# RWKV block inverses through DRAM: scratch laid out by row, block, column, each matrix read back with one transfer

## The chip, the core and the metric

The kernel runs on one core of a Trainium2 chip. The metric is the device time of one execution in microseconds (us). TensorE is called PE here (PEld is its weight load), VectorE DVE, ScalarE ACT, GpSimd POOL, and SP is the engine whose queue issues most DMAs.

## The reference

Two layers of a decoder trunk are computed in float32 on 512 tokens of width 1024. Each layer has a SwiGLU half-step, a mixer (four FoX attention heads, eight RWKV-7 heads, four MoBA heads), a cross attention and a second half-step. The change lies in RWKV-7, whose recurrence is:

```python
def step(state, inp):
    r_t, w_t, k_t, v_t, kk_t, a_t = inp
    sa = jnp.einsum('bhij,bhj->bhi', state, -kk_t)
    state = (state * w_t[:, :, None, :] + sa[..., None] * (kk_t * a_t)[:, :, None, :]
             + v_t[..., None] * k_t[:, :, None, :])
    return state, jnp.einsum('bhij,bhj->bhi', state, r_t)
...
_, ys = lax.scan(step, state0, xs)
```

## The kernel before

**Chunks.** The recurrence is worked in 8 chunks of 64 tokens, for two heads at a time. A pair of heads is called `hp` (0 to 3), so with two layers there are eight episodes, called e0 to e3 (first layer) and e4 to e7 (second layer) below. In each, 16 unit-triangular matrices of 64x64 (8 chunks by 2 heads) have to be inverted.

**Through DRAM.** `rwkv_gram` makes these matrices in the tile `G` (DVE, L721). They are written to a DRAM scratch `scA` (L726, two transfers). From there the four 16x16 blocks on each diagonal are read into `A16` (L730, four transfers), so that the 64 partitions of `A16` hold 4 places by 16 matrices. POOL inverts all of these by back substitution, 30 instructions at L282, and makes a transposed copy (L742). Eight transfers (L746) put the 16x16 inverses on the diagonals of two other scratches that hold zeros elsewhere: `scT` for the transposes, `scP` for the inverses. Then the whole 64x64 matrices come back as `Tf` and `Pf`, tiles of 128 partitions (two heads of 64 rows) by 8 chunks by 64 columns. Each is read at L749 with two transfers of 64 partitions, 128 KB each. All of these transfers are issued by SP, in order, and so are the weight loads (L130), 512 KB each into a ring of three buffers `wraw`.

**After it.** `rwkv_inverse` goes from 16x16 to 64x64 with small matmuls: L809 reads `Tf`, L818 and L826 read `Pf`. PE works strictly in the order of its instructions, so what stands behind L809 waits when L809 waits. Projections (L152 to L154, L948 to L950) fill PE between these steps. Every weight block is split by ACT (`whi`, L145) and DVE (`wlo`, L146) before use.

**The order.** The sequence of the parts is the string `ORDER` and a table of priorities. From these a scheduler sets the order of the instructions on each engine, with its own estimate of how long each takes. So an edit of a transfer can move instructions on engines that it does not touch.

Of the kernel before, what the change touches and what calls it, by code (L numbers as in the profile page):

```python
# [6 lines left out]
F32 = mybir.dt.float32  # L7
# [8 lines left out]
P = 128  # L16
# [75 lines left out]
H = (slice(0, 64), slice(64, 128))  # L92
# [23 lines left out]
class Trunk:  # L116
# [304 lines left out]
    def make_scratch(self, tmp):  # L421

        z = tmp.tile([P, S], F32, name="zs", tag="zs")
        self.nc.gpsimd.memset(z, 0.0)
        self.scA = [self.tc.dram_tile([2, 8, 64, 64], F32, name=f"scA{i}") for i in range(2)]
        self.scP = [self.tc.dram_tile([2, 8, 64, 64], F32, name=f"scP{i}") for i in range(2)]
        self.scT = [self.tc.dram_tile([2, 8, 64, 64], F32, name=f"scT{i}") for i in range(2)]
        for sc in self.scP + self.scT:
            self.nc.gpsimd.dma_start(sc.rearrange("h c s t -> (h c s t)").rearrange("(p n) -> p n", p=P), z)

    def derive_params(self, const):
        nc = self.nc
# [269 lines left out]
    def rwkv_gram(self, l, hp, st):  # L702

        nc, rw = self.nc, self.rw
        ps = lambda c=8: self.bank(TAGS["g"], c)
        mm = nc.tensor.matmul
        ER, B = st["ER"], st["B"]

        G = st["G"] = rw.tile([P, 16, 64], F32, name="G", tag="G")

        BN = st["BN"] = rw.tile([P, 8, 4, 64], F32, name="BN", tag="BN")
        for q in range(2):
            pg = [ps(4).rearrange("p c (i t) -> p c i t", i=2) for h in range(2)]
            for c in range(4):
                g, i = 2 * q + c // 2, c % 2
                for h in range(2):
                    mm(pg[h][:, c].rearrange("p i t -> p (i t)"), B[H[h], g, 2 * i:2 * i + 2].rearrange("p a b -> p (a b)"),  # L717
                       ER[H[h], g, 1:3] if i == 0 else ER[H[h], g, 0:4:3], start=True, stop=True)
            for h in range(2):
                for i, dst in ((0, G[:, 8 * h + 4 * q:8 * h + 4 * q + 4]), (1, BN[:, 4 * q:4 * q + 4, 1 + h])):  # L720
                    nc.vector.tensor_tensor(dst, pg[h][:, :, i], self.gmask[:, i:i + 1, :].to_broadcast([P, 4, 64]), op=ALU.mult)  # L721
            yield

        scA, scP, scT = (x[hp % 2] for x in (self.scA, self.scP, self.scT))
        for a in range(2):
            nc.sync.dma_start(scA[a].rearrange("j s t -> s j t"), G[H[a], 1 - a::2])  # L726
        A = rw.tile([64, 16, 16], F32, name="A16", tag="A16")
        for q in range(4):
            d = slice(16 * q, 16 * q + 16)
            nc.sync.dma_start(A[d], scA.rearrange("a j s t -> (a j) s t")[:, d, d])  # L730
        I = rw.tile([64, 16, 16], F32, name="P16", tag="P16")
        tmp = rw.tile([64, 16, 16], F32, name="T16", tag="T16")
        If = I.rearrange("p a b -> p (a b)")
        nc.gpsimd.memset(If, 0.0)
        nc.gpsimd.memset(If[:, 0:256:17], 1.0)
        for u in range(15, 0, -1):
            n = 16 - u
            self.tt("sub", tmp[:, 0:u, 0:n], A[:, 0:u, u:u + 1].to_broadcast([64, u, n]),
                    I[:, u:u + 1, u:16].to_broadcast([64, u, n]), ALU.mult)
            self.tt("sub", I[:, 0:u, u:16], I[:, 0:u, u:16], tmp[:, 0:u, 0:n], ALU.subtract)  # L740
        It = rw.tile([64, 16, 16], F32, name="I16", tag="T16")
        nc.gpsimd.tensor_copy(It, I.rearrange("p a b -> p b a"))  # L742
        for name, sc, src in (("Tf", scT, It), ("Pf", scP, I)):
            for q in range(4):
                d = slice(16 * q, 16 * q + 16)
                nc.sync.dma_start(sc.rearrange("a j s t -> (a j) s t")[:, d, d], src[d])  # L746
            st[name] = rw.tile([P, 8, 64], F32, name=name, tag=name)
            for a in range(2):
                nc.sync.dma_start(st[name][H[a]], sc[a].rearrange("j s t -> s j t"))  # L749
        yield  # L750

    def rwkv_rows(self, l, hp, st):
# [604 lines left out]
```

## Time and profile before

| | |
|---|---|
| median of 3 runs | 2575.36 us (2575.05 to 2586.14) |
| the profiled execution's own time | 2590.88 us |
| its span | 2589.1 us |
| mean granted TensorE clock | 0.974 |
| busy share of the span | PE 96%, PEld 78%, DVE 52%, ACT 33%, POOL 19% |
| DMA packets | 434880, 218.41 MB |

A busy share says how long an engine had an instruction in work. The granted clock is the share of TensorE's full speed that the chip allowed. Its two levels are 1.2 and 2.4 GHz, which the rows show as 0.50 and 1.00. A wait is put down to the instruction or transfer that ended last before the waiting instruction began.

### The profile page before, as it was taken

The numbers are of one execution on the slowest core, as the hardware profiler recorded it, in microseconds if no ns is written. First come the engines' busy times: TensorE is split into PE (matmuls) and PEld (weight loads), VectorE is DVE, ScalarE is ACT, GpSimd is POOL, SyncE is SP. The second block draws the span as 40 slices with busy tenths as digits, with TensorE's granted clock in tenths as the row PEclk, the third lists the DMA queues.
The fourth block names the chain that finished last, engine by engine and source line by source line (L and its number), as shares of the span: only waits on it lengthen the run. The fifth ranks groups of instructions, "written<-read, shape, count | busy, mean of one in ns | idle before, by whom it ended". The sixth has DMA issues, their size and how long they took to land.

```text
span 2589.1 us, 35163 instructions
## 1 busy us (share of the span) xinstructions
PE 2497.2 (96%) x13976; PEld 2025.7 (78%) x13976; DVE 1346.6 (52%) x2503; ACT 846.9 (33%) x1337; POOL 493.0 (19%) x610
## 2 busy tenths in 40 slices
PE   8999998899999899999999999999999899999999
PEld 7888876787667788888888888767877677888887
DVE  6444445666755654344444444465666666543444
ACT  4222233233343342222332222333333433422222
POOL 4212120232210122020221211202322110221211
PEclk9999999998889999999999999999978999999999
DMA  4333342221213133333333333422212121333332
GB/s 143 104 98 94 96 130 69 66 59 43 64 34 92 53 96 90 104 93 98 95 94 100 94 98 94 121 75 58 67 34 56 56 78 45 110 98 98 95 95 88
DMA packets 434880, 218.41 MB, mean 84 GB/s; under 512 B 63856, under 2 KB 428828, under 8 KB 434716
## 3 DMA queue, kind: packets, MB, share of 16 engines
q1 hardware_dynamic: 431948, 212.36, 28.9%
q10 hardware_dynamic: 2448, 2.76, 0.3%
q8 instruction: 110, 1.80, 0.3%
q0 software_dynamic: 320, 1.05, 0.1%
q14 instruction: 54, 0.44, 0.1%
HBM read 205.64 MB, written 10.49 MB: 83 GB/s over the span
## 4 chain that ended last, share of the span: by engine, by line
PE 86%; DVE 6%; POOL 3%; DMA 2%; ACT 2%; issue 1%; SPq 1%; POOLq 0%; ACTq 0%; DVEq 0%
PE acc L152 22%; PE acc L154 22%; PE acc L153 22%; PE po L1046 2%; PE sp L1034 1%; POOL P L282 1%; PE pt L1022 1%; PE acc L950 1%; PE acc L948 1%; PE acc L949 1%; POOL T L282 1%; DVE wlo L146 1%; ACT whi L145 1%; PE ts L857 1%; PE ty L717 1%
## 5 line engine op out<-in xcount | busy, mean ns | idle before, releaser
L145 ACT ACTIVATE whi<-wraw 128x1024 fp32r<-128x1024 f32 (+3 forms) x386 | 390.3, 1013 | 1142.0 <-PE acc L153 1043.3
L152 PE MATMUL acc<-xh,whi 128*128 128x512 f32 (+1 forms) x1776 | 699.9, 394 | 21.9 <-DVE p L496 7.3
L154 PE MATMUL acc<-xh,wlo 128*128 128x512 f32 (+1 forms) x1776 | 695.8, 392 | 1.3 <-DVE wlo L146 1.3
L153 PE MATMUL acc<-xl,whi 128*128 128x512 f32 (+1 forms) x1776 | 694.8, 391 | 0.0
L146 DVE TENSOR_TENSOR wlo<-wraw,whi 128x1024 fp32r<-128x1024 f32 (+3 forms) x386 | 540.3, 1401 | 100.3 <-ACT whi L145 91.4
L152 PEld LDWEIGHTS acc<-xh,whi 128*128 128x128 f32 (+1 forms) x1776 | 334.4, 188 | 97.6 <-ACT whi L145 9.1
L154 PEld LDWEIGHTS acc<-xh,wlo 128*128 128x128 f32 (+1 forms) x1776 | 334.2, 188 | 75.5 <-DVE wlo L146 2.6
L153 PEld LDWEIGHTS acc<-xl,whi 128*128 128x128 f32 (+1 forms) x1776 | 334.6, 188 | 69.7
L342 POOL TENSOR_TENSOR up<-up,g 128x512 f32<-128x512 f32 x88 | 118.4, 1346 | 999.2 <-ACT whi L145 901.1
L152 PE MATMUL acc<-th,whi 128*128 128x512 f32 x704 | 274.4, 391 | 1.0 <-ACT whi L145 1.0
L154 PE MATMUL acc<-th,wlo 128*128 128x512 f32 x704 | 275.0, 392 | 0.2
L153 PE MATMUL acc<-tl,whi 128*128 128x512 f32 x704 | 274.0, 389 | 0.0
L295 DVE SCALAR_TENSOR_TENSOR x<-acc,x 128x512 f32<-128x512 f32 x96 | 66.0, 691 | 277.2 <-PE acc L154 277.2
L341 DVE TENSOR_TENSOR up<-acc,rsb 128x512 f32<-128x512 f32 x88 | 60.8, 691 | 278.5 <-PE acc L154 278.5
L338 DVE TENSOR_TENSOR g<-acc,rsb 128x512 f32<-128x512 f32 x88 | 60.8, 691 | 191.0 <-PE acc L154 188.0
L154 PEld LDWEIGHTS acc<-th,wlo 128*128 128x128 f32 x704 | 132.1, 188 | 31.5 <-DVE wlo L146 4.2
L152 PEld LDWEIGHTS acc<-th,whi 128*128 128x128 f32 x704 | 132.2, 188 | 30.5 <-ACT whi L145 4.0
L153 PEld LDWEIGHTS acc<-tl,whi 128*128 128x128 f32 x704 | 132.2, 188 | 27.4
L240 POOL TENSOR_TENSOR sqacc<-sqacc,sq 128x512 f32<-128x512 f32 x48 | 75.4, 1571 | 381.6 <-ACT sq L239 245.9
L346 POOL TENSOR_TENSOR tl<-up,th 128x512 fp32r<-128x512 f32 x88 | 128.5, 1461 | 65.5 <-ACT th L345 65.5
L345 ACT ACTIVATE th<-up 128x512 fp32r<-128x512 f32 x88 | 55.8, 634 | 120.8 <-POOL up L342 120.8
L948 PE MATMUL acc<-whi,xh 128*128 128x256 f32 x256 | 76.9, 300 | 0.7 <-DVE zt L520 0.7
(351 smaller groups left out, 3109.1 us busy)
## 6 DMA issues: line engine op xcount, KB each, us to landing
wraw<-in_ffn_w_in_dram SPq DMA_DIRECT2D x176, 512.0 KB
wraw<-in_ffn_w_out_dram SPq DMA_DIRECT2D x64, 512.0 KB
wraw<-in_mix_w_in_dram SPq DMA_DIRECT2D x52, 512.0 KB
wraw<-in_ffn_w_out_dram SPq DMA_DIRECT2D x32, 384.0 KB
wraw<-in_xattn_w_kv_dram SPq DMA_DIRECT2D x16, 512.0 KB
wraw<-in_mix_w_out_dram SPq DMA_DIRECT2D x16, 384.0 KB
scx<-x SPq DMA_DIRECT2D x16, 256.0 KB
x<-scx SPq DMA_DIRECT2D x16, 256.0 KB
```

What stands on the lines that cost most here:

```text
L145: nc.scalar.activation(hv, v, AF.Copy)
L146: nc.vector.tensor_sub(lv, v, f32(hv))
L152: mm(ps, lh, rh, start=start, stop=False)
L153: mm(ps, lh, rl, start=False, stop=False)
L154: mm(ps, ll, rh, start=False, stop=stop)
L240: (nc.vector if m == KC - 1 else nc.gpsimd).tensor_tensor(self.sqacc, self.sqacc, sq, op=ALU.add)
L295: self.nc.vector.scalar_tensor_tensor(xm, ps, coef, xm, op0=ALU.mult, op1=ALU.add)
L338: nc.vector.tensor_tensor(g, pss[0], rsb, op=ALU.mult)
L341: nc.vector.tensor_tensor(up, pss[1], rsb, op=ALU.mult)
L342: nc.gpsimd.tensor_tensor(up, up, g, op=ALU.mult)
L346: nc.gpsimd.tensor_tensor(tl, up, f32(th), op=ALU.subtract)
L948: mm(o, a, wh[:, kk, :], start=k == 0, stop=False)
```

## The change

All scratches get the layout row, block, column: `[64, 16, 64]` instead of `[2, 8, 64, 64]`. The writes and the reads of the 16x16 blocks address the same bytes in the new places, with as many transfers and the same 64-byte runs. The writes of `scA` stay two. Each of `Tf` and `Pf` is read with one transfer of 128 partitions by 2 KB instead of two transfers of 64 partitions by 8 runs of 256 bytes. The source of that transfer is addressed as head, row, run: outermost 2, then 64, then 512 contiguous floats. The destination is 128 partitions by 512 floats.

```diff
-        self.scA = [self.tc.dram_tile([2, 8, 64, 64], F32, name=f"scA{i}") for i in range(2)]
-        self.scP = [self.tc.dram_tile([2, 8, 64, 64], F32, name=f"scP{i}") for i in range(2)]
-        self.scT = [self.tc.dram_tile([2, 8, 64, 64], F32, name=f"scT{i}") for i in range(2)]
+        self.scA = [self.tc.dram_tile([64, 16, 64], F32, name=f"scA{i}") for i in range(2)]
+        self.scP = [self.tc.dram_tile([64, 16, 64], F32, name=f"scP{i}") for i in range(2)]
+        self.scT = [self.tc.dram_tile([64, 16, 64], F32, name=f"scT{i}") for i in range(2)]
...
         for a in range(2):
-            nc.sync.dma_start(scA[a].rearrange("j s t -> s j t"), G[H[a], 1 - a::2])
+            nc.sync.dma_start(scA[:, 8 * a:8 * a + 8], G[H[a], 1 - a::2])
...
-            nc.sync.dma_start(A[d], scA.rearrange("a j s t -> (a j) s t")[:, d, d])
+            nc.sync.dma_start(A[d], scA[d, :, d].rearrange("s j t -> j s t"))
...
-                nc.sync.dma_start(sc.rearrange("a j s t -> (a j) s t")[:, d, d], src[d])
+                nc.sync.dma_start(sc[d, :, d].rearrange("s j t -> j s t"), src[d])
             st[name] = rw.tile([P, 8, 64], F32, name=name, tag=name)
-            for a in range(2):
-                nc.sync.dma_start(st[name][H[a]], sc[a].rearrange("j s t -> s j t"))
+            nc.sync.dma_start(st[name].rearrange("p j t -> p (j t)"), sc.rearrange("s (a j) t -> a s (j t)", a=2))
```

In the changed file every line behind L748 has a number lower by one, so that L808 is the old L809 and L817 the old L818.

SP's queue in e0, from the writes of the inverses to the weight load behind the reads, before:

```order
L746 DMA scP_376<-P_3333 16x16x16 x3
L746 DMA scT_378<-I_3367 16x16x16 x4
L746 DMA scP_376<-P_3333 16x16x16
L749 DMA Tf<-scT_378 64x8x64 x2
L749 DMA Pf<-scP_376 64x8x64 x2
L130 DMA wraw<-in_mix_w_in_dram 128x4x256
```

And the same place in the changed kernel:

```order
L746 DMA scP_376<-P_3333 16x16x16 x3
L746 DMA scT_378<-I_3367 16x16x16 x4
L746 DMA scP_376<-P_3333 16x16x16
L748 DMA Tf<-scT_378 128x1x512
L748 DMA Pf<-scP_376 128x1x512
L130 DMA wraw<-in_mix_w_in_dram 128x4x256
```

The four reads have become two, and nothing else moved here.

PE in e1, from the first matmul that reads `Tf` on (`tk` is the operand made of `G`, `gs` and `g` belong to the output gate of e0), before:

```order
L809 MATMUL ty<-Tf,tk_4123 64x64
L948 MATMUL acc<-whi,xh 128x256
L949 MATMUL acc<-whi,xl 128x256
L950 MATMUL acc<-wlo,xh 128x256
L809 MATMUL ty<-Tf,tk_4123 64x64 x15
L924 MATMUL ts<-ident,tk_4379 128x128 x4
L930 MATMUL ts<-gs_2923,g_4335 128x512
L931 MATMUL ts<-gs_2962,g_4335 128x512
L672 MATMUL tx<-ident,e 128x128 x4
L948 MATMUL acc<-whi,xh 128x256
```

And the same place in the changed kernel:

```order
L808 MATMUL ty<-Tf,tk_4119 64x64 x16
L947 MATMUL acc<-whi,xh 128x256
L948 MATMUL acc<-whi,xl 128x256
L949 MATMUL acc<-wlo,xh 128x256
L923 MATMUL ts<-ident,tk_4375 128x128 x4
L929 MATMUL ts<-gs_2923,g_4331 128x512
L930 MATMUL ts<-gs_2962,g_4331 128x512
L672 MATMUL tx<-ident,e 128x128 x4
L817 MATMUL ty<-tk_4139,Pf 32x16 x16
L825 MATMUL ty<-Pf,tk_4139 64x32 x16
```

All matmuls that read `Tf` now stand together at the front, and those that read `Pf` follow at once. Before, eleven projection matmuls of 128x256 stood between L672 and L818.

SP's queue in e3, before (the first row is two weight loads, of the cross attention's keys and values):

```order
L130 DMA wraw<-in_xattn_w_kv_dram 128x8x128 x2
L746 DMA scP_377<-P_5536 16x16x16 x3
L746 DMA scT_379<-I_5570 16x16x16 x4
L746 DMA scP_377<-P_5536 16x16x16
L749 DMA Tf<-scT_379 64x8x64 x2
L749 DMA Pf<-scP_377 64x8x64 x2
```

And the same place in the changed kernel:

```order
L130 DMA wraw<-in_xattn_w_kv_dram 128x8x128
L746 DMA scP_377<-P_5530 16x16x16 x3
L746 DMA scT_379<-I_5564 16x16x16 x4
L746 DMA scP_377<-P_5530 16x16x16
L130 DMA wraw<-in_xattn_w_kv_dram 128x8x128
L748 DMA Tf<-scT_379 128x1x512
L748 DMA Pf<-scP_377 128x1x512
```

One weight load of 512 KB has moved from ahead of the writes to just ahead of the reads.

## Rows read from the trace of the kernel before

**Rows 1.** The page: the shares of the span that the chain of work that ended last spent, by engine.

```profile
PE 86%; DVE 6%; POOL 3%; DMA 2%; ACT 2%; issue 1%; SPq 1%; POOLq 0%; ACTq 0%; DVEq 0%
```

**Rows 2.** The waits of PE over the whole span: waiting line, what released it, us in total, how often, the longest.

```profile
PE ty L809 <- DMA Tf<-scT: 9.4, 6, 3.9
```

**Rows 3.** The chain of work that ended last, in order of time, around the read of `Tf` in e0: start, us, what (a DMA counts from its issue to the work that it releases).

```profile
494.36 3.00 DMA Tf<-scT
...
497.40 0.69 PE ty L809 x7
```

**Rows 4.** The timeline of SP's queue: the issues of `Tf`'s two transfers in each of the eight episodes e0 to e7 (start, us until both are issued).

```profile
493.71 1.28 SPq L749 DMA_DIRECT2D Tf<-scT  x2
...
568.49 1.28 SPq L749 DMA_DIRECT2D Tf<-scT  x2
...
628.75 1.29 SPq L749 DMA_DIRECT2D Tf<-scT  x2
...
702.49 1.27 SPq L749 DMA_DIRECT2D Tf<-scT  x2
...
1774.60 1.28 SPq L749 DMA_DIRECT2D Tf<-scT  x2
...
1848.93 1.28 SPq L749 DMA_DIRECT2D Tf<-scT  x2
...
1907.49 1.28 SPq L749 DMA_DIRECT2D Tf<-scT  x2
...
1980.63 1.28 SPq L749 DMA_DIRECT2D Tf<-scT  x2
```

**Rows 5.** The timeline of PE: where the matmuls that read `Tf` (L809) and the first that read `Pf` (L818) begin, with PE's idle time before them in brackets, in e0 to e7.

```profile
496.64 0.33 PE L809 MATMUL ty<-Tf,tk 64*64 64x64 f32 x2 [2.52 <-DMA Tf<-scT]
497.40 0.91 PE L809 MATMUL ty<-Tf,tk 64*64 64x64 f32 x12 [0.43 <-DMA Tf<-scT]
506.64 0.68 PE L818 MATMUL ty<-tk,Pf 32*32 32x16 f32 x32
...
571.42 0.29 PE L809 MATMUL ty<-Tf,tk 64*64 64x64 f32 x2 [1.11 <-DMA Tf<-scT]
577.66 0.68 PE L818 MATMUL ty<-tk,Pf 32*32 32x16 f32 x32
...
637.98 0.32 PE L809 MATMUL ty<-Tf,tk 64*64 64x64 f32 x2
643.38 0.68 PE L818 MATMUL ty<-tk,Pf 32*32 32x16 f32 x32
...
708.70 1.97 PE L809 MATMUL ty<-Tf,tk 64*64 64x64 f32 x32
711.65 0.86 PE L818 MATMUL ty<-tk,Pf 32*32 32x16 f32 x32
...
1778.28 1.01 PE L809 MATMUL ty<-Tf,tk 64*64 64x64 f32 x14 [0.41 <-DMA Tf<-scT]
...
1851.83 0.30 PE L809 MATMUL ty<-Tf,tk 64*64 64x64 f32 x2 [1.04 <-DMA Tf<-scT]
...
1920.44 0.33 PE L809 MATMUL ty<-Tf,tk 64*64 64x64 f32 x2
...
1986.21 1.15 PE L809 MATMUL ty<-Tf,tk 64*64 64x64 f32 x32
```

**Rows 6.** The DMA view: the queue of the transfers that ACT issues (packets, MB, share of 16 engines), and all transfers issued on it (count, KB each).

```profile
q10 hardware_dynamic: 2448, 2.76, 0.3%
...
mtk<-in_mem_dram ACTq DMA_DIRECT2D x2, 1024.0 KB
...
lw<-in_rwkv_w_dram ACTq DMA_DIRECT2D x8, 32.0 KB
lw<-in_rwkv_a_dram ACTq DMA_DIRECT2D x8, 32.0 KB
...
gm<-in_moba_q_gain_dram ACTq DMA_DIRECT2D x2, 32.0 KB
gm<-in_moba_k_gain_dram ACTq DMA_DIRECT2D x2, 32.0 KB
...
fb<-in_fox_f_bias_dram ACTq DMA_DIRECT2D x2, 0.0 KB
...
pstage<-in_ffn_norm_dram ACTq DMA_DIRECT2D x1, 8.0 KB
```

**Rows 7.** Stretches with DMA traffic: us, busy time of each engine (instructions), granted clock, mean busy share of the 16 DMA engines, GB/s. First eight loads of `x` (128 partitions by 2 KB each), then one store of the same shape, then the reads of `Tf` and `Pf` in e0 (256-byte runs).

```profile
758.00:763.00 5.00, 5.00 (x33) 3.99 (x31) 1.67 (x6) 2.85 (x10) 2.99 (x3) 0.81 0.96 329
...
374.12:374.92 0.80, 0.80 (x5) 0.64 (x5) 0.71 (x2) 0.41 (x1) 0.31 (x1) 1.00 0.84 325
...
495.00:498.00 3.00, 0.93 (x14) 0.79 (x16) 2.69 (x13) 0.00 (x0) 0.10 (x1) 0.85 0.82 181
```

**Rows 8.** The same view for the stretch behind PE's wait in e0 and for the one behind its wait in e1 (granted clock is the third number from the end).

```profile
497.00:504.00 7.00, 6.60 (x41) 5.52 (x42) 1.22 (x6) 0.60 (x1) 0.00 (x0) 0.51 0.62 174
...
574.00:580.00 6.00, 6.00 (x88) 4.32 (x87) 4.82 (x8) 0.74 (x1) 1.38 (x1) 1.00 0.18 54
```

**Rows 9.** From the timeline of ACT in e0, the split of a weight block, and from the chain of work in order of time, one projection matmul of 128x256 (start, us, what).

```profile
516.84 1.06 ACT L145 ACTIVATE whi<-wraw 128x1024 fp32r<-128x1024 f32 x1 [0.97 <-PE acc L153]
...
518.74 0.12 PE acc L948
```

More of the change, by code (lines that the diff above doesn't have):

```diff
@@ L424, in make_scratch @@
         self.nc.gpsimd.memset(z, 0.0)
-        self.scA = [self.tc.dram_tile([2, 8, 64, 64], F32, name=f"scA{i}") for i in range(2)]
-        self.scP = [self.tc.dram_tile([2, 8, 64, 64], F32, name=f"scP{i}") for i in range(2)]
-        self.scT = [self.tc.dram_tile([2, 8, 64, 64], F32, name=f"scT{i}") for i in range(2)]
+        self.scA = [self.tc.dram_tile([64, 16, 64], F32, name=f"scA{i}") for i in range(2)]
+        self.scP = [self.tc.dram_tile([64, 16, 64], F32, name=f"scP{i}") for i in range(2)]
+        self.scT = [self.tc.dram_tile([64, 16, 64], F32, name=f"scT{i}") for i in range(2)]
         for sc in self.scP + self.scT:
-            self.nc.gpsimd.dma_start(sc.rearrange("h c s t -> (h c s t)").rearrange("(p n) -> p n", p=P), z)
+            self.nc.gpsimd.dma_start(sc.rearrange("s j t -> (s j t)").rearrange("(p n) -> p n", p=P), z)
     def derive_params(self, const):
```

## The prediction

> **What bounds the kernel now.** First the page: PE is 86% of the chain that ended last, DMA 2% [rows 1]. So a transfer counts only where PE stands still for it. The waits of PE show how often that is: L809 waits for `Tf` in 9.4 us altogether [rows 2]. The chain around e0 shows how the wait is made up: the second of the two transfers is issued at 494.36, lands 3.00 us later, and L809 goes on at 497.40 [rows 3]. The timelines of SP and PE then give the slack of each episode. In e0, e1, e4 and e5 PE is there before `Tf` (idle 2.52 and 0.43 in e0, 1.11 in e1, similar in the second layer). In e2, e3, e6 and e7 L809 starts without a wait, 9.2, 6.2, 13.0 and 5.6 us behind the first issue [rows 4, 5]. L818, which needs `Pf`, waits nowhere.
>
> **What is removed.** Per episode two issues of some 0.64 us on SP (1.28 for a pair [rows 4]), and, for each matrix, 896 of 1024 packets (128 runs of 2 KB in place of 1024 of 256 bytes). If nothing else changed, `Tf` would be whole one issue earlier: the start of the chain moves from 494.36 to 493.71 in e0. That is the gain that the first rival below has in full.
>
> **What the new read costs.** The question is over how many DMA engines it is spread. The ACT queue shows how that is decided. Its transfers have 2 x 256 runs of `mtk`, 16 x 64 rows of `lw`, 4 x 128 rows of `gm`, 16 rows of `pstage` and 2 x 4 floats of `fb`: 2072 pieces. The queue counts 2448 packets [rows 6]. The 376 left over are 23 x 16 + 2 x 4. I read them as one completion mark for each engine used: sixteen for every transfer of 16 rows or more, but four for `fb`, whose outermost count is 4. With sixteen for each the queue would count 2472. So a transfer is dealt out by the outermost dimension, and one with a short outermost dimension runs on few engines. The new read has 2 outermost in its source and 128 in its destination. Two source entries can be dealt to two engines, so I take two. No row shows a transfer with unequal counts; that is what is uncertain.
>
> The Trainium skill states the rule for just that case (DMA: Bandwidth & Descriptors, section on why a DMA increments its semaphore by 16 and not by 1): the number of engines is the largest one up to 16 that divides the outermost count of both sides, which gives two here. The count of `fb` agrees; the unequal case is shown by no run so far. By that rule the sum below stands as it is; by the other rule of that page it would be the first rival's.
>
> On two engines each carries 128 KB of `Tf`, then 128 KB of `Pf`, since SP issues them one after the other into the same queue. The rate of one engine with 2 KB runs: 329 GB/s over 16 x 0.96 is 21.4 GB/s for loads, 325 over 16 x 0.84 is 24.2 for stores [rows 7]. I take the middle, 22.8, because two engines press on the memory less than sixteen at 96%: 131072 B are 5.75 us. The fixed part of a read is 3.00 less the data part now: 8 KB per engine at 181/(16 x 0.82) = 13.8 GB/s [rows 7], 0.6 us, so 2.4. **`Tf` is there 8.2 us behind the first issue, `Pf` 13.9 us**, instead of about 3.7 for `Tf`.
>
> PE's added idle time for `Tf`, ready time against the start that the rows give [rows 4, 5]:
> - e0: 493.71 + 8.2 = 501.9 against 497.40: 4.5. e4: 1774.60 + 8.2 against 1778.28: 4.5.
> - e1: 576.7 against 571.42: 5.3. The three matmuls that lay between the halves of `Tf` before now stand behind it, so all of it is idle. e5: 1857.1 against 1851.83: 5.3.
> - e2: 636.95 against 637.98, where the new order asks some 1.6 us earlier (thirteen projection matmuls of 128x256, at 0.12 us each [rows 9], no longer stand ahead of it): 0.6. e6: 1915.7 against 1920.44: 0.
> - e3: 710.7 against 708.70, asked 0.7 us earlier in the new order (six such matmuls): 2.7. Here a weight load now stands ahead of the reads on SP. It is 32 KB per engine, at 21.4 GB/s 1.5 us if the read lies wholly behind it, 0 if it is over; I take 0.8. e7: 1988.8 against 1986.21, 2.6.
>
> Together 26.3 us. `Pf` comes into play where L818 follows soon after L809. In e0 it is ready at 507.6, and L818 would stand at 506.64 + 4.5: no wait. In e1 it is ready at 582.4 and wanted at 577.66 + 5.3 - 1.3 (the eleven matmuls that moved behind it [rows 9]) = 581.7: 0.7. In e3 it is ready at 717.2 and wanted at 711.65 + 3.5: 2.0. The second layer is taken as the first: 5.4 us in all.
>
> **The clock.** Behind PE's wait in e0 the granted clock is 0.51 over 7 us (the level of 1.2 GHz), so 3.4 us of work are lost there; behind the wait of 1.11 in e1 it stays at 1.00 [rows 8]. With 5.3 us of idle time I expect e1 and e5 to lose the same, and e7 too; e3 ran on a low clock already, which the 1.97 us of its L809 against 1.15 in e7 shows [rows 5]. Three stretches are 10.2 us. While PE is slow it comes to L818 later, so the 3.4 us of waits for `Pf` in e1, e5 and e7 are within this: 6.8 more. If no stretch is added, it is nothing.
>
> **At nothing.** Weight loads issued behind the reads share the two queues and land up to 11 us later; the first one behind e0's reads (issued at about 496.4) is the next but one to be split, at 516.84 [rows 9], 20 us on, so I count none of it. If that cover were gone, it would cost up to those 11 us an episode. The writes of the blocks keep their count and run length; their new addresses could cost nothing, or at most double a data part of 0.6 us in each of three steps, 1.8 us in each of the four episodes that PE waits for. I take nothing. The moves of instructions are work that PE does in either order.
>
> **Sum.** 26.3 + 5.4 + 6.8 = 38.5 us. The profiled execution took 2590.88 us, 15.5 above the median of the runs; the difference is made within the one execution, and I add it to the median: 2575.4 + 38.5 = **2614 us**, 1.5% slower.
>
> **The rivals.**
> - *Spread over sixteen engines* (dealt by the 128 partitions of the destination). Each engine has 16 KB, 0.75 us, so `Tf` is ready 3.2 us behind the first issue: 496.9 instead of 497.4 in e0. In e0, e1, e4 and e5 PE gains 0.5 us each: 2573 us, no change that can be told. For it: each of the 128 rows goes to a partition of its own, and all large transfers of before run on sixteen. Against it: the marks of `fb`. The Trainium skill has a rule that would give this time (DMA: Bandwidth & Descriptors, Rules for kernel authors): two transfers to disjoint halves of the partitions gain nothing over one of 128. In this kernel it would hold if the one transfer kept its sixteen engines.
> - *Sixteen engines and the clock held.* The same 0.5 us earlier, and the idle time of e0 and e4 gets short enough that their two low stretches of 3.4 us do not come: 2575.4 - 2 - 6.8 = 2567, on the other side of before. It decides if PE's wait in e0 falls from 2.95 us to something like the 1.11 of e1, at which the clock stayed. Half a microsecond does not do that.
> - *Two engines, but hidden.* PE would have to have other work ahead of L809. The order gives it less: in e1, e2 and e3 L809 and L818 stand earlier. Only e2 and e6 hide it. With the fast rate of 24.2 and no clock stretch the sum is still about 27 us: 2602.
>
> **How the numbers follow.** 0.5% (12.9 us) is about what a measurement of this kernel can tell from no change. Two engines: 0.79, nearly all of it slower; its own range is 2598 (fast rate, no clock) to 2630 (21.4 GB/s, a stretch more, late weight loads). Sixteen engines: 0.17, no change. Faster: 0.04. The range that leaves out no more than 2 in 10 reaches down to the second case: 2572 to 2632. Slower 0.78, same 0.18, faster 0.04.
>
> **What would show it.** In the profile after, L808 waits for `Tf` some 35 us instead of 9.4, in all but e2 and e6, and the DMA view shows a low busy share with long duration during the reads (2 of 16 engines, 0.13 plus other traffic). From the issue of `Tf` to L808 in e0 it is 8 us; 3.2 would make the step on the two engines wrong, and with it the forecast. The packets, 434880 before, fall by 16 x 896 = 14336 for the reads; with them go 32 x 16 = 512 completion marks, and 16 x 2 = 32 come if the reads run on two engines, 256 if on sixteen: 14816 fewer in all, or 14592. The granted clock behind e1 and e5 is at 0.50 for some 7 us; if it stays at 1.00, that term is wrong. If other waits of PE shrink as L808's grows, the sum is too large.

## The result and the profile after

| | before | changed |
|---|---|---|
| median | 2580.75 us (4 runs, 2575.05 to 2596.5) | 2620.35 us (4 runs, 2606.84 to 2626.09) |
| profiled execution: own time, span | 2590.88, 2589.1 us | 2626.09, 2624.4 us |
| mean granted clock | 0.974 | 0.968 |

The ratio of the runs is 1.0142, with a 95% interval of 1.0112 to 1.0172: the change makes the kernel 1.4% slower. (The two medians of the table alone differ by 39.6 us, 1.5%.)

The page of the changed kernel, the count of packets and the chain that ended last by engine (against [rows 1]):

```profile
DMA packets 420065, 218.42 MB, mean 83 GB/s; under 512 B 46992, under 2 KB 411964, under 8 KB 419900
...
PE 86%; DVE 4%; DMA 4%; POOL 2%; ACT 2%; issue 1%; SPq 1%; ACTq 0%; POOLq 0%; DVEq 0%
```

DMA has doubled its share of the chain, from 2% to 4%. The packets fell by 434880 - 420065 = 14815.

The waits of PE in the changed kernel (waiting line, what released it, us in total, how often, the longest); the first line answers to [rows 2]:

```profile
PE ty L808 <- DMA Tf<-scT: 34.8, 6, 8.7
...
PE ty L817 <- DMA Pf<-scP: 5.2, 2, 3.1
```

The wait for `Tf` went from 9.4 to 34.8 us, and a wait for `Pf` is new. The chain in order of time around the read of `Tf` in e0 (answers to [rows 3]):

```profile
498.57 8.12 DMA Tf<-scT
...
506.73 1.33 PE ty L808 x19
```

The timeline of PE, with the idle time before an instruction in brackets: the first matmuls that read `Tf` (L808) and, where they waited, those that read `Pf` (L817), in e0 to e5 and e7 (answers to [rows 5]):

```profile
506.73 1.97 PE L808 MATMUL ty<-Tf,tk 64*64 64x64 f32 x32 [7.91 <-DMA Tf<-scT]
...
585.83 1.97 PE L808 MATMUL ty<-Tf,tk 64*64 64x64 f32 x32 [6.73 <-DMA Tf<-scT]
...
647.76 1.15 PE L808 MATMUL ty<-Tf,tk 64*64 64x64 f32 x32
...
716.30 1.97 PE L808 MATMUL ty<-Tf,tk 64*64 64x64 f32 x32 [3.16 <-DMA Tf<-scT]
721.49 0.68 PE L817 MATMUL ty<-tk,Pf 32*32 32x16 f32 x32 [2.17 <-DMA Pf<-scP]
...
1806.97 1.97 PE L808 MATMUL ty<-Tf,tk 64*64 64x64 f32 x32 [8.71 <-DMA Tf<-scT]
...
1885.65 1.98 PE L808 MATMUL ty<-Tf,tk 64*64 64x64 f32 x32 [6.53 <-DMA Tf<-scT]
...
2015.45 1.15 PE L808 MATMUL ty<-Tf,tk 64*64 64x64 f32 x32 [1.80 <-DMA Tf<-scT]
2020.64 1.04 PE L817 MATMUL ty<-tk,Pf 32*32 32x16 f32 x32 [3.06 <-DMA Pf<-scP]
```

PE waits for `Tf` in every episode but e2 (its row has no bracket) and e6. The duration behind the start shows the clock: 1.97 us for the 32 matmuls at the lower level, 1.15 at the upper.

Where the time went is read from stretches: us, busy time of PE, PEld, DVE, ACT and POOL (instructions), granted clock, DMA share, GB/s. First before, from the first write of `scA` in a layer to that layer's cross attention, for layer 1 and layer 2:

```profile
467.80:889.20 421.40, 396.31 (x3147) 313.50 (x3147) 259.21 (x674) 150.36 (x302) 84.74 (x166) 0.93 0.22 60
...
1747.20:2172.10 424.90, 398.69 (x3147) 319.44 (x3147) 258.01 (x675) 150.33 (x302) 83.19 (x165) 0.92 0.22 60
```

The same stretches of the changed kernel, and then the times around and behind PE's waits in e0 and e1:

```profile
472.50:913.80 441.30, 402.30 (x3147) 320.36 (x3147) 258.10 (x674) 149.96 (x302) 85.81 (x166) 0.90 0.21 57
...
1771.90:2207.30 435.40, 396.63 (x3146) 315.80 (x3146) 258.26 (x675) 149.64 (x302) 83.92 (x165) 0.92 0.21 58
...
499.00:507.00 8.00, 0.27 (x5) 0.27 (x6) 3.79 (x14) 0.58 (x1) 0.45 (x3) 0.63 0.37 105
...
501.00:511.00 10.00, 4.27 (x38) 3.67 (x39) 1.79 (x10) 0.60 (x1) 0.10 (x1) 0.51 0.47 138
...
583.00:589.00 6.00, 3.17 (x38) 3.08 (x39) 0.00 (x0) 0.81 (x2) 0.00 (x0) 0.50 0.35 111
```

The two stretches grew by 441.3 - 421.4 = 19.9 and 435.4 - 424.9 = 10.5 us, 30.4 of the 35.3 by which the span grew. Length less PE's busy time is its idle time: 25.1 to 39.0 and 26.2 to 38.8, together 26.5 us more. The other 3.9 us are busy time (6.0 more in layer 1, 2.1 less in layer 2), the same instructions at a lower or higher clock. The last 4.7 us of the span lie ahead of the first write of `scA`, where both kernels have the same transfers and instructions in the same order; they are no effect of the change, and show how far two executions differ by themselves. During the read of e0 PE worked 0.27 of 8 us, and the DMA engines had a share of only 0.37.

### The profile page after: what moved, and what is told of

Its sections match the earlier page's. It is cut to its first block, busy times and chain, and to the rows that moved or that the text cites. A ratio compares the mean times of both kernels' runs of the same rounds, so it can differ in the third digit from the quotient of the medians.

```text
span 2624.4 us, 35148 instructions
## 1 busy us (share of the span) xinstructions
PE 2507.0 (96%) x13976; PEld 2033.6 (77%) x13976; DVE 1347.9 (51%) x2503; ACT 845.7 (32%) x1337; POOL 493.1 (19%) x610
## 2 busy tenths in 40 slices
DMA packets 420065, 218.42 MB, mean 83 GB/s; under 512 B 46992, under 2 KB 411964, under 8 KB 419900
## 4 chain that ended last, share of the span: by engine, by line
PE 86%; DVE 4%; DMA 4%; POOL 2%; ACT 2%; issue 1%; SPq 1%; ACTq 0%; POOLq 0%; DVEq 0%
PE acc L152 22%; PE acc L154 22%; PE acc L153 22%; PE po L1045 2%; DMA Tf<-scT 1%; PE sp L1033 1%; PE acc L947 1%; PE acc L948 1%; PE pt L1021 1%; PE acc L949 1%; ACT whi L145 1%; DMA Pf<-scP 1%; PE ts L856 1%; POOL P L282 1%; DVE wlo L146 1%
```

## The experiments

**One transfer of 128 rows on sixteen engines.** The changed kernel has a new order, one transfer for two, and (by the forecast) two engines for sixteen. This run keeps the first two (the order nearly; in SP's queue a weight load now stands between the two reads of e0) and addresses the source as 128 runs in the order of their addresses, so that the rows land in other partitions.

```diff
-            nc.sync.dma_start(st[name].rearrange("p j t -> p (j t)"), sc.rearrange("s (a j) t -> a s (j t)", a=2))
+            nc.sync.dma_start(st[name].rearrange("p j t -> p (j t)"), sc.rearrange("s j t -> (s j t)").rearrange("(p n) -> p n", p=P))
```

> The changed kernel, but each of Tf and Pf is read as 128 contiguous pieces of 2 KB, one per partition: still one transfer, same size, same run length, same place in SP's queue and nearly the same order on PE; only the source's outermost count is 128 instead of 2. The rows land in other partitions than they should, so the numbers that come out are not the reference's. Theory (two outermost entries in the source mean two DMA engines): with 128 the transfer runs on sixteen again, the time from the issue of Tf to L808 in e0 falls from 8.1 us to about 3.2, PE waits for Tf 7 to 8 us in all instead of 34.8, for Pf nothing, and the time is 0.997 to 1.001 of the kernel before. Rival (one long transfer in place of two is slow by itself): 8 us and 1.014 stay. Rival (the new order on PE, which this kernel keeps, is what costs): L808's wait shrinks but the time stays near 1.01.

Measured: 2570.01 us, ratio 0.995 (0.9925 to 0.9974). PE's wait for `Tf`; SP's issue of it in e0 and the matmuls that read it (timelines); 7 us at the end of PE's wait in e0 and in e4, and the stretches of the two layers:

```profile
PE ty L808 <- DMA Tf<-scT: 6.4, 4, 3.4
```

```profile
497.81 0.34 SPq L748 DMA_DIRECT2D Tf<-scT  x1
```

```profile
500.44 1.15 PE L808 MATMUL ty<-Tf,tk 64*64 64x64 f32 x32 [0.60 <-DMA Tf<-scT]
```

```profile
500.00:507.00 7.00, 6.56 (x70) 5.33 (x72) 3.81 (x14) 1.20 (x2) 0.10 (x1) 1.00 0.60 183
1775.00:1782.00 7.00, 6.08 (x47) 5.18 (x48) 1.58 (x8) 0.60 (x1) 0.00 (x0) 0.76 0.64 206
...
473.60:888.10 414.50, 394.41 (x3145) 312.34 (x3146) 258.20 (x674) 149.73 (x302) 84.48 (x166) 0.93 0.22 61
1746.30:2160.20 413.90, 389.87 (x3146) 310.11 (x3147) 258.31 (x674) 149.77 (x302) 84.14 (x165) 0.95 0.22 61
```

From issue to L808 it is 500.44 - 497.81 = 2.63 us here against 8.16 in the changed kernel, with the same 2 KB runs and as many transfers; the packets are 420289, 224 more than in the changed kernel, which is 16 reads by 14 marks. So neither one transfer, nor the layout, nor the order costs anything: the slow part is the address with 2 outermost. And there is something that the forecast had almost at nothing: this kernel beats the one before by 0.5%. By the stretches of the two layers PE's idle time is 7.2 us less than before (51.3 to 44.1) and its busy time 10.7 less (795.0 to 784.3). Behind e0's wait, which is 0.60 us instead of 2.95, the clock is 1.00, where [rows 8] had 0.51. In e4 PE still waits the 3.4 us that the first row ends with, and the clock there is 0.76.

By the stretches of the two layers, PE's idle time in the changed kernel is 39.0 + 38.8 = 77.8 us, here 20.1 + 24.0 = 44.1, and its busy time 798.9 against 784.3. In these single executions the two engines cost 33.7 us of idle time and 14.6 of clock, 48.3 in all; by the ratios (1.0142 against 0.995) it is 1.9%.

**Two transfers of 64 partitions in the new layout.** The same 2 KB runs, each row in its place, and 64 outermost on both sides.

```diff
-            nc.sync.dma_start(st[name].rearrange("p j t -> p (j t)"), sc.rearrange("s (a j) t -> a s (j t)", a=2))
+            for a in range(2):
+                nc.sync.dma_start(st[name][H[a]], sc[:, 8 * a:8 * a + 8])
```

> The new layout with all its writes, but Tf and Pf are each read with two transfers of 64 partitions by 2 KB, whose source and destination both have 64 outermost. Theory: sixteen engines each, Tf whole about 3.8 us after the first issue in e0 (two issues of 0.6, 2.4 fixed, 0.4 of data for the second half), PE waits for Tf about 9 us in all, and the time is 0.997 to 1.002 of the kernel before. Rival (the new layout is the cause: rows 4 KB apart, blocks written 256 bytes and 4 KB apart): Tf takes about 8 us and the time stays near 1.014, or the writes and the read of A16 show longer times than before.

Measured: 2573.32 us, ratio 0.9962 (0.9939 to 0.9984), which beats both kernels. The wait for `Tf`; issue and matmuls in e0 (timelines of SP and PE; L502 is the work that PE does ahead of them); the 7 us behind:

```profile
PE ty L809 <- DMA Tf<-scT: 5.7, 7, 1.7
```

```profile
495.04 1.14 SPq L749 DMA_DIRECT2D Tf<-scT  x2
```

```profile
496.51 0.72 PE L502 MATMUL sp<-blk,p 128*128 128x2 f32 x6
497.62 0.32 PE L809 MATMUL ty<-Tf,tk 64*64 64x64 f32 x2 [0.39 <-DMA Tf<-scT]
498.51 1.14 PE L809 MATMUL ty<-Tf,tk 64*64 64x64 f32 x30 [0.25 <-DMA Tf<-scT]
```

```profile
497.00:504.00 7.00, 6.36 (x56) 5.31 (x56) 4.28 (x15) 1.82 (x3) 0.10 (x1) 1.00 0.76 205
```

Both halves are there 3.47 us behind the first issue, and again the clock stays at 1.00 behind e0's wait. Compared with one transfer of 128 rows it is 0.9962 to 0.995, within the intervals. The Trainium skill has a rule on this (DMA: Bandwidth & Descriptors, Rules for kernel authors): two transfers to disjoint halves of the partitions gain nothing over one of 128, because both run on the same engines. These two runs agree; in the changed kernel, whose one transfer does not keep sixteen engines, it did not hold.

**Four engines.** If the outermost count sets the engines, 4 outermost must lie between. The scratches of the inverses get a gap behind every 16 rows, so that the source of each half is 4, 16, 512 floats; PE's instructions stand as in the run before.

```diff
-        self.scT = [self.tc.dram_tile([64, 16, 64], F32, name=f"scT{i}") for i in range(2)]
+        self.scT = [self.tc.dram_tile([4, 17, 16, 64], F32, name=f"scT{i}") for i in range(2)]
...
+            for a in range(2):
+                nc.sync.dma_start(st[name][H[a]].rearrange("p j t -> p (j t)"), sc[:, 0:16, 8 * a:8 * a + 8].rearrange("q r j t -> q r (j t)"))
```

> As the kernel with two halves, in the same order on PE, but the two scratches are padded (4 groups of 17 rows, 16 used), so that each half's source has 4 outermost, then 16 rows of 2 KB. Theory: four engines, each with 64 KB of Tf, 2.9 us at 22.8 GB/s: Tf ready 5.3 us after the first issue, Pf 8.1. PE waits 1.6 us longer than with sixteen in each of e0, e1, e4 and e5, and a little in e3 and e7: 6 to 10 us, ratio 1.002 to 1.005, between the kernel with two halves and the changed one. The marks add up to 4 for each of the 32 reads. Rival (dealt out by the 64 partitions of the destination, or only a count of 2 is special): as the kernel with two halves, 3.8 us and 1.000.

Measured: 2597.61 us, ratio 1.0051 (1.0024 to 1.0077), 0.9% above the run before. Waits of PE, SP's issue in e0, and the matmuls:

```profile
PE ty L809 <- DMA Tf<-scT: 15.3, 10, 2.5
...
PE ty L818 <- DMA Pf<-scP: 0.7, 1, 0.7
```

```profile
496.94 1.21 SPq L749 DMA_DIRECT2D Tf<-scT  x2
```

```profile
500.94 0.33 PE L809 MATMUL ty<-Tf,tk 64*64 64x64 f32 x2 [1.77 <-DMA Tf<-scT]
502.49 1.96 PE L809 MATMUL ty<-Tf,tk 64*64 64x64 f32 x30 [0.91 <-DMA Tf<-scT]
```

Both halves are there 5.55 us behind the first issue in e0, and 5.2 to 5.9 in e0, e1, e4 and e5. The packets are 420160, 384 fewer than with 64 outermost: 32 transfers by 12 marks. So the time goes with the number of engines: 2.6 to 2.9 us on sixteen for one transfer of 256 KB (where PE waited for it), 5.2 to 5.9 on four (two transfers of 128 KB), 8.0 to 9.1 on two. This is the rule on unequal outermost counts that the forecast cited from the Trainium skill (DMA: Bandwidth & Descriptors, section on why a DMA increments its semaphore by 16 and not by 1); the marks counted here, 2, 4 and 16 a transfer, agree with it in each case.

**`Tf` on sixteen engines, `Pf` on two.** This parts the cost of `Tf` from that of `Pf`. `Tf` is read in halves, `Pf` as in the changed kernel.

```diff
+            if name == "Tf":
+                for a in range(2):
+                    nc.sync.dma_start(st[name][H[a]], sc[:, 8 * a:8 * a + 8])
+            else:
+                nc.sync.dma_start(st[name].rearrange("p j t -> p (j t)"), sc.rearrange("s (a j) t -> a s (j t)", a=2))
```

> New layout; Tf is read in two halves on sixteen engines, Pf with the one transfer of the changed kernel. It parts the cost of the two reads. Theory: Tf whole 3.8 us after its first issue, so PE waits for it about 9 us in all as before; Pf is whole about 9.5 us after Tf's first issue and is wanted some 8 to 10 us after it in e1, e3, e5 and e7: waits for Pf of 1 to 2 us in some of these, 2 to 6 us in all; ratio 1.000 to 1.003. Rival (late weight loads behind the two-engine read, not the waits for Tf and Pf, make a good part of the loss): the ratio stays above 1.006 with L808's wait at 9 us, and PE waits longer for whi and wlo.

Measured: 2590.12 us, ratio 1.0022 (1.0 to 1.0044), 0.6% above the run with both in halves. Waits of PE (L812 is the old L809, L821 the old L818):

```profile
PE acc L152 <- ACT whi L145: 9.0, 16, 1.0
...
PE ty L812 <- DMA Tf<-scT: 7.4, 5, 2.7
PE ty L821 <- DMA Pf<-scP: 6.0, 4, 2.1
```

The issue of `Tf` and PE's work around its wait in e0 (timelines), and the 7 us behind the wait:

```profile
497.17 1.14 SPq L750 DMA_DIRECT2D Tf<-scT  x2
```

```profile
496.56 0.72 PE L502 MATMUL sp<-blk,p 128*128 128x2 f32 x6
500.01 0.47 PE L812 MATMUL ty<-Tf,tk 64*64 64x64 f32 x2 [2.72 <-DMA Tf<-scT]
```

```profile
500.00:507.00 7.00, 6.99 (x44) 5.88 (x45) 3.87 (x14) 0.60 (x1) 0.10 (x1) 0.51 0.58 173
```

With `Pf` alone slow, PE waits for it in e1, e3, e5 and e7, 6.0 us in all; so of the 1.9% that two engines cost for both, `Pf` is the smaller part (0.6%). The first row is PE's wait for a split weight block. It is 9.0 us in 16 waits before, in the changed kernel, and in the three runs above alike: the weight loads behind the reads cost nothing.

The rows of e0 also show how little one episode of one execution proves. Up to the issue of `Tf` this kernel and the one with both reads in halves have the same transfers and instructions in the same order, and they read `Tf` alike. They write `scA` at 471.19 and 471.14 us and reach L502 at 496.56 and 496.51. But the steps between, through `scA`, POOL and the scratches, take 26.0 us here and 23.9 there, so that `Tf` is issued at 497.17 and 495.04. PE's wait is 2.72 us here and 0.64 there, and the clock behind it 0.51 here and 1.00 there. The short wait in e0 is thus not by itself a mark of the new reads.

**The layout alone.** Is the gain of the first two runs one of the layout? Here the new layout is kept but each block is followed by a gap of 64 floats, so that the halves are read in 256-byte runs again. PE and SP then have the order of the kernel before, row for row.

```diff
-        self.scT = [self.tc.dram_tile([64, 16, 64], F32, name=f"scT{i}") for i in range(2)]
+        self.scT = [self.tc.dram_tile([64, 16, 128], F32, name=f"scT{i}") for i in range(2)]
...
+            for a in range(2):
+                nc.sync.dma_start(st[name][H[a]], sc[:, 8 * a:8 * a + 8, 0:64])
```

> The new layout, but with the blocks of the two scratches that are read back 128 floats apart, so that the reads (two halves each, 64 outermost, sixteen engines) move runs of 256 bytes as before. The order on PE and in SP's queue is then that of the kernel before, row for row. It asks what the layout is worth by itself. Theory (the layout is worth nothing, the kernel with two halves gained 0.4% by the order on PE that came with 2 KB runs): 3.7 us from the issue of Tf to the second group of L809 in e0, PE waits for Tf 9 to 10 us in all, ratio 0.998 to 1.002. Rival (the layout makes the writes or the read of A16 faster): the ratio is as with two halves, 0.994 to 0.998, and L809's wait is well below 9 us.

Measured: 2589.06 us, ratio 1.0014 (0.9994 to 1.0034). Issue and matmuls in e0, the 7 us behind PE's wait, and the wait for `Tf` over the whole span (9.4 us before):

```profile
500.48 1.28 SPq L749 DMA_DIRECT2D Tf<-scT  x2
```

```profile
503.63 0.33 PE L809 MATMUL ty<-Tf,tk 64*64 64x64 f32 x2 [1.58 <-DMA Tf<-scT]
504.32 1.95 PE L809 MATMUL ty<-Tf,tk 64*64 64x64 f32 x30 [0.36 <-DMA Tf<-scT]
```

```profile
503.00:510.00 7.00, 6.01 (x45) 5.06 (x46) 3.02 (x13) 0.60 (x1) 0.10 (x1) 0.76 0.74 199
```

```profile
PE ty L809 <- DMA Tf<-scT: 8.8, 6, 3.6
```

The layout is worth nothing by itself, as far as this run can show it: `scA` has the addresses of the changed kernel, while the blocks of the other two scratches lie 512 bytes apart and not 256. What the halves gained comes with the 2 KB runs and the order that they bring. In e0 both halves are there 3.84 us behind the first issue (3.47 with 2 KB runs, 3.69 before). When PE asks for them, e0 does not settle: 1.57 us behind the issue here and 0.41 before, in one order; 2.19 with both in halves and 0.12 with `Tf` alone in halves, in the other. Which is worth more, the shorter reads or the order, no run separates.

**What the change set out to do, on sixteen engines.** One transfer for each matrix with 128 outermost and each row in its place needs the two heads apart in the scratch, and then twice as many writes. To keep SP's queue short, the writes of `scP` and the read of `Pf` are issued by ACT.

```diff
-        self.scT = [self.tc.dram_tile([64, 16, 64], F32, name=f"scT{i}") for i in range(2)]
+        self.scT = [self.tc.dram_tile([2, 64, 8, 64], F32, name=f"scT{i}") for i in range(2)]
...
+            q_ = nc.sync if name == "Tf" else nc.scalar
...
+                for a in range(2):
+                    q_.dma_start(sc[a, d, :, d].rearrange("s j t -> j s t"), src[16 * q + 8 * a:16 * q + 8 * a + 8])
...
+            q_.dma_start(st[name].rearrange("p j t -> p (j t)"), sc.rearrange("a s j t -> (a s) (j t)"))
```

> What the change set out to do, on sixteen engines: scratches for Tf and Pf laid out by head, row, block, column, so that one transfer reads 128 contiguous rows of 2 KB. The 16x16 blocks must then be written head by head, 8 partitions at a time, sixteen writes a matrix instead of eight; those of scP and the read of Pf are issued by ACT, so that SP issues no more than before. Theory: 2.7 us from the issue of Tf to L809 in e0, as with 128 contiguous rows; ratio 0.993 to 0.998. Rival (ACT, which works in order, is held up by eight issues of 0.45 us and by their wait for POOL, and the splits of weights behind them come late): L809 no longer waits for Tf, but PE waits longer for ACT, and the ratio is 1.000 or more.

Measured: 2604.97 us, ratio 1.0083 (1.0058 to 1.0107). PE no longer waits for `Tf` at all. ACT's waits and its timeline in e0, and one of PE's waits, which no run above has (L949 is the old L948):

```profile
ACT KV L275 <- DMA scP<-P: 24.7, 4, 7.3
...
ACT yn L927 <- DMA scP<-P: 12.9, 2, 6.8
```

```profile
488.00 2.30 ACTq L748 DMA_DIRECT2D scP<-P  x6
490.40 1.06 ACT L145 ACTIVATE whi<-wraw 128x1024 fp32r<-128x1024 f32 x1 [8.43 <-DMA scP<-P]
```

```profile
PE acc L949 <- ACT whi L145: 2.6, 2, 1.4
```

Like PE, ACT did what it issues and computes in order here: the writes wait for POOL's inverses, so ACT stands 8.43 us ahead of a split that PE's projections need, and over 37 us in the eight episodes in two of its waits alone. PE in turn waits for splits at L949, and its idle time over the span is 2596.9 - 2497.6 = 99.3 us, against 2586.0 - 2498.4 = 87.6 with two halves: the gain of the read is lost. The doubled writes have 8 outermost on both sides, and the packets are 420289, as with one transfer of 128 rows: 128 writes with 8 marks each have as many marks as 64 with 16.

**The same issues by ACT, without the doubled writes.** The halves of the second run, with only the writes of `scP` and the reads of `Pf` moved to ACT.

```diff
+            q_ = nc.sync if name == "Tf" else nc.scalar
...
-                nc.sync.dma_start(sc[d, :, d].rearrange("s j t -> j s t"), src[d])
+                q_.dma_start(sc[d, :, d].rearrange("s j t -> j s t"), src[d])
...
+                q_.dma_start(st[name][H[a]], sc[:, 8 * a:8 * a + 8])
```

> The kernel with two halves, with the writes of scP and the reads of Pf issued by ACT instead of SP. Tf's path on SP loses three issues of 0.45 us ahead of it. Theory: the issue of Tf comes about 1 us earlier after POOL's transposed copy in e0, e1, e4 and e5, PE's wait for Tf falls to 2 to 5 us, ratio 0.992 to 0.996. Rival (six to eight DMA issues on ACT hold up its evictions and weight splits): the ratio is 0.997 or more and PE waits longer for ACT.

Measured: 2604.03 us, ratio 1.0076 (1.0049 to 1.0103). PE's wait for `Tf`, and ACT in e0:

```profile
PE ty L810 <- DMA Tf<-scT: 8.0, 4, 3.5
```

```profile
492.27 1.06 ACT L145 ACTIVATE whi<-wraw 128x1024 fp32r<-128x1024 f32 x1 [7.25 <-DMA scP<-P]
```

It takes as long as the run above, so the doubled writes need not be what costs there: with the issues moved to ACT alone the kernel is 1.1% over the same halves issued by SP. The move also brings another order on PE, so that ACT's standing still is the likely cause, but not shown to be the only one.

## Why the prediction was right, and where it was not

**The engines.** The step on which all rested held: `Tf` was used 8.12 us behind its issue in e0 (forecast 8.2), and the packets fell by 14815 (forecast 14816 for two engines, 14592 for sixteen). The three runs with 4, 64 and 128 outermost show that it was this count and nothing else in the edit. That the 8.2 came so close is in part luck, because its two terms were off in opposite ways. On sixteen engines, with 16 KB each, the read took 2.63 us, on two, with 128 KB each, 8.16; the 112 KB between them took 5.53 us. That is an estimate of 20.7 GB/s for one engine, where the forecast took 22.8, and it leaves 1.8 us for the fixed part, where it took 2.4.

**PE's waits.** By episode, the whole wait for `Tf`, forecast (the wait before, of [rows 5] and for e4 the 4.3 that is left of the 9.4, plus the added idle time) against measured: e0 7.5 and 7.9, e1 6.4 and 6.7, e2 0.6 and 0, e3 3.5 and 3.2, e4 8.8 and 8.7, e5 6.3 and 6.5, e6 0 and 0, e7 2.6 and 1.8. The total was 35.7 against 34.8. `Pf` was right in sum, 5.4 against 5.2, and half right in place: nothing in e1 and e5, 2.17 and 3.06 in e3 and e7.

**Other waits shrank.** The forecast named this as what would make its sum too large, and it did: 25.4 more for `Tf` and 5.2 for `Pf` are 30.6, but PE's idle time in the two layers grew by 26.5. Elsewhere PE waits some 4 us less than before.

**The clock.** The three stretches that were forecast came: 0.50 over the 6 us shown for e1, where [rows 8] had 1.00; in e5 L808 took 1.98 us, the lower level's duration; and in e7 L817 took 1.04 us where e3's took 0.68. But others moved or went, and in the sum the clock was worth 3.9 us of busy time, not 6.8.

**So the sum** of 38.5 stands against 30.4 us that the traces show in the two layers; the 35.3 by which the spans differ come nearer only through the 4.7 us ahead of the first change. The runs' ratio, 1.1 to 1.7%, is 29 to 44 us and holds both. The 2598 us at the low end of the forecast's own range do not agree with its third rival, which puts the same case (fast rate, no clock) at 2602; nothing hangs on it.

**The step that failed** is what the rest of the edit is worth. It hides behind the cost of the two engines. The forecast gave a read on sixteen engines 2 us (2573 us, 0.9991) and the new order nothing: "The moves of instructions are work that PE does in either order." Measured are 0.995 and 0.9962. The layout alone is not it (1.0014), so the 2 KB runs, the order that comes with them, or both are worth 0.4 to 0.5%; which, and by what wait, stays open. The rival *sixteen engines and the clock held*, 2567 us or 0.9967 of 2575.4, has about the right time, but its mechanism is only half seen. With one transfer and with two halves the clock held behind e0's wait. In e4, behind waits of 3.38 and 1.92 us, it was 0.76 over 7 us in both (0.51 before, behind 4.26 us). And e0's waits were short in good part because `Tf` was issued sooner behind the first write of `scA`: 24.25 and 23.90 us, against 25.91 before and 25.98 in the run with `Tf` alone in halves, whose wait was long again. So "Half a microsecond does not do that" is not refuted by these rows. What stands is that the changed kernel loses more to its two engines, some 48 us, than it shows against the kernel before.

## What to carry to other kernels

When an access pattern is rearranged to make one transfer of two, look at its outermost count: a head or half of 2 in front of the source put the whole transfer on two engines here, although it filled 128 partitions. Keep the long dimension outermost, by two transfers if need be. (A short count on the destination alone was not tried.) A read that PE waits for is priced by bytes per engine and not by bytes. And a transfer that waits for another engine holds up what stands behind it on the engine that issues it. An engine whose other work is waited for, as ACT's splits are here, is a poor place for it. Last, a single wait in a single execution, such as that of e0, can change by 2 us with nothing edited ahead of it; a gain of half a percent needs more than that to be explained.

## What the runs showed of the hardware

- The completion marks in the count of packets tell how many engines a transfer used, to the last one: 16 x 14 = 224 between one transfer on sixteen and on two, 32 x 12 = 384 between halves on sixteen and on four. Writes with 8 outermost on both sides left 8 marks each.
- One or two microseconds at one wait can decide over several at the lower clock: behind e0's wait the granted clock was 1.00 after 0.60 and 0.64 us of idle time, 0.76 after 1.94, 0.51 after 2.72 and 0.51 after 2.95 [rows 5, 8], each over the next 7 us. These are single executions of five kernels, and no limit can be read from them: in e4 of the kernel with one transfer of 128 rows it was 0.76 at a wait of 3.38 us.
- The reads of 2 KB runs on sixteen engines were faster than forecast: 2.63 us from issue to use in e0 (2.6 to 2.9 where PE waited) in place of 3.2.
